# Input x handed over feature-major in column blocks; squares summed by products with ones, 1/rms multiplied in by VectorE and GpSimd; another order of the head

## The chip, the core and the metric

One Trainium2 chip, one of its cores. The metric is the device time of one execution in microseconds (us), the median of the runs shown. The engines are called as the profile calls them: PE (TensorE matmul), PEld (its weight load), DVE (VectorE), ACT (ScalarE), POOL (GpSimd), SP (SyncE, here only a queue of DMA issues). DVE, ACT and PE reach both on-chip memories, SBUF and PSUM; in this kernel POOL works on SBUF tiles only.

## The reference, cut to what matters

One decoder layer on 1024 prompt rows and 64 sample rows (8 sequences of 8), 1088 columns of work in all, 1024 features. What the change touches is the first line: the RMS norm of x, and the modulation by scale and shift, which come from a small product of the conditioning c with `w_ada`.

```python
shift, scale, gate = silu(c) @ w_ada + b_ada
h = x * rsqrt(mean(x * x, axis=-1) + 1e-6) * norm_g * (1 + scale) + shift
u_pool, z_pool, z_ssm, xBC, dt, g = split(h @ w_in)
P = (pool_mix(u_pool) * silu(z_pool)) @ w_pool_out
S = gated_rmsnorm(SSD(conv(xBC)) + D * xs, z_ssm) @ w_ssm_out
x = x + gate * ((sigmoid(g_pool) * P + sigmoid(g_ssm) * S) @ w_o)
y = rmsnorm(x, final_g)
```

All is float32. Large products are made of three products of halves: every operand is split into a rounded part ("hi") and the rest ("lo"), and hi*hi, hi*lo and lo*hi are summed in PSUM.

## The kernel before

h is wanted feature-major: 8 tiles k = 0..7 of 128 features (partitions) by 1088 columns, since the products with `w_in` sum over features. x arrives row-major. The 1088 columns are worked in three blocks, `BLK`: block 0 is 256 wide, block 1 384, block 2 448 (384 prompt columns and the 64 sample columns).

The head, `first()` (L837 and on), does the following. Nine loads bring x (L197, 128 rows each; the ninth is the 64 sample rows). `x_square` sums the squares of a row, on DVE (L204) or ACT (L206), into a column of `ss`; `x_root` (L210) and `x_unit` (L214) make 1/rms of 128 rows in one number per partition, and L219 puts these on the diagonal of a 128x128 matrix. `x_turn` (L231) multiplies a piece of x by that diagonal on PE: this turns the piece to feature-major and scales it at once. `x_copy` (L239 DVE, L241 ACT) brings it from PSUM into the tiles `tf[k]`. There are 64 pieces of 128x128 and 8 of 64 rows.

Beside this, `ada_load`, `ada_mm` (L277), `ada_out` (L284) and `ada_end` (L292 to L299) make shift and scale into the table `md`, in three parts: k 0 and 1, k 2 and 3, k 4 to 7. `h_make(block, ks)` makes h in place: for each k a rounded part on ACT (L323, for block 2 L332), the exact one on ACT for odd k (L325) or DVE for even k (L327), the rest `low` on DVE (L315). The sample columns have a scale and shift of their own for every sequence, two DVE operations of 64 columns per k (L330, L331). `products(block, ks)` (L866 to L868) are the first products with `w_in`: two column tiles of the gates g, whose weights `w_load` brings and `w_split` (L163 ACT, L166 DVE or POOL) splits. All of h and of these products done, `combine()` makes sums of h's quarters for the Strassen-like pairs that follow (L497 to L500 and others), `dt_block` (L727) makes dt, `gate_load` and `gate_mm` (L817, L823) make the gate of the residual. `gate_bias` (L827, L829) clears a tile `bg` on POOL and loads a bias into it; the gate loads stand behind these four loads on SP. Then the first pair starts (L595 to L597), and from there the same loop of pairs fills PE for the rest.

Order: `in_line` chains the instructions of `first()` on PE, ACT, DVE, POOL and SP in the order in which the code was written, so each of these queues runs the head exactly as written, one instruction behind the other, whatever is ready. Only the weights of the pairs (the L540 operations on DVE) are put between by the scheduler.

Of the kernel before, what the change touches and what calls it, by code (L numbers as in the profile page):

```python
# [8 lines left out]
F32 = mybir.dt.float32  # L9
# [11 lines left out]
P = 128  # L21
# [31 lines left out]
@with_exitstack  # L53
def tile_pool_ssd_step(
    ctx: ExitStack, tc: tile.TileContext,
    x_prompt, x_sample, state_pool, state_conv, state_ssm, state_turned, c_all,
    w_ada, b_ada, feat_vecs, w_in, w_first, w_dt, conv_vecs, dt_bias, a_log, skip_vecs,
    pool_w, w_pool_out, w_ssm_out, w_o, final_g,
    y_prompt, y_sample, new_pool_p, new_conv_p, new_ssm_p, new_pool_s, new_conv_s, new_ssm_s,
# [51 lines left out]
    def const(shape, name, dt=F32):  # L111
        return cp.tile(shape, dt, tag=name, name=name)
# [72 lines left out]
    xr = []
    xbig = [Y4(hs, F32), Y4(hs, F32)]
    ss = const([P, 9], "ss")
    nc.gpsimd.memset(ss, 1.0)
    rs = const([P, 9], "rs")
    dg = []  # L190
    hh_ = [None] * KT
    hl_ = [None] * KT

    def x_load(i):
        n = P if i < 8 else NS
        xt = R([P, D]) if i == 8 else xbig[i // 4][:, i % 4, :D]
        load(xt[:n], x_prompt[0, i * P:(i + 1) * P, :] if i < 8 else x_sample.rearrange("b t d -> (b t) d"))  # L197
        xr.append((xt, n))

    def x_square(i, eng):  # L200
        xt, n = xr[i]
        sqj = pa.tile([P, D], F32, tag="rawA", name=nm("sqj"), bufs=5)
        if eng is V:
            V.scalar_tensor_tensor(sqj[:n], xt[:n], 1.0, xt[:n], ALU.mult, ALU.mult, accum_out=ss[:n, i:i + 1])  # L204
        else:
            act(sqj[:n], xt[:n], AF.Square, accum_out=ss[:n, i:i + 1])  # L206

    def x_root(a, b):
        n = xr[a][1]
        act(rs[:n, a:b], ss[:n, a:b], AF.Sqrt, bias=eps[:n], scale=1.0 / D)  # L210

    def x_unit(a, b):
        n = xr[a][1]
        V.reciprocal(rs[:n, a:b], rs[:n, a:b])  # L214
        if not dg:
            dg.append(R())
        for i in range(a, b):
            n = xr[i][1]
            V.tensor_scalar(dg[0][:n, i * P:i * P + n], ident[:n, :n], rs[:n, i:i + 1], None, ALU.mult)  # L219

    tf = [None] * KT

    def x_turn(g3, k):

        if g3 == 0:
            tf[k] = tfp.tile([P, T], F32, tag="tf", name=nm("tf"), bufs=8)
        px = PB()
        c = 0
        for i in range((0, *XG)[g3], XG[g3]):
            xt, n = xr[i]  # L230
            mm(px[:, c:c + n], xt[:n, k * P:(k + 1) * P], dg[0][:n, i * P:i * P + n], start=True, stop=True)  # L231
            c += n
        return g3, k, px, c

    def x_copy(turned, eng):
        g3, k, px, c = turned
        o = BLK[g3][0]
        if eng is V:
            V.tensor_copy(tf[k][:, o:o + c], px[:, :c])  # L239
        else:  # L240
            act(tf[k][:, o:o + c], px[:, :c], AF.Copy)  # L241

    def x_turns(g3, ks):
        for k in ks:
            x_copy(x_turn(g3, k), nc.scalar if k % 2 else V)


    PARTS = ((0, 2), (2, 4), (4, 8))
# [3 lines left out]
    def ada_load(part, k):  # L252
        a, b = PARTS[part]
        w = (b - a) * P
        if part == 0:
            if k == 0:
                wtile[0] = Y4(hp, F32)
            t = wtile[0][:, k // 2, :D]
        else:
            if part == 2 or k % 2 == 0:  # L260
                wtile[part, k] = G((P, D))
            t = wtile[part, k if part == 2 else k - k % 2]
        if part == 2:
            load(t, w_ada[8 + k])
        else:
            if k % 2 == 0:
                load(t, w_ada[4 * part + k // 2])
            t = t[:, k % 2 * 512:k % 2 * 512 + 512]
        wraw[part, k] = t.rearrange("p (s c) -> p s c", s=2)
# [34 lines left out]
    def h_tile(k, j):  # L304
        if not hb:
            hb.extend(Y4(hp) for _ in range(2))
        return hb[j][:, k] if k < 4 else G((P, T), F32R)

    def h_make(g3, ks):

        o, w = BLK[g3]
        e = min(o + w, SEQ) - o

        def low(k):
            V.tensor_tensor(hl_[k][:, o:o + w], tf[k][:, o:o + w], hh_[k][:, o:o + w].bitcast(F32), ALU.subtract)  # L315
        for k in ks:
            if hh_[k] is None:
                hh_[k], hl_[k] = h_tile(k, 0), h_tile(k, 1)
            t = tf[k][:, o:o + w]
            hi = hh_[k][:, o:o + w]  # L320
            sc, sh = md[:, 8 + k], md[:, k]
            if e == w:
                act(hi, t, AF.Identity, scale=sc[:, 0:1], bias=sh[:, 0:1])  # L323
            if k % 2:
                act(t[:, :e], t[:, :e], AF.Identity, scale=sc[:, 0:1], bias=sh[:, 0:1])  # L325
            else:
                V.tensor_scalar(t[:, :e], t[:, :e], sc[:, 0:1], sh[:, 0:1], ALU.mult, ALU.add)  # L327
            if e < w:
                ts_ = t[:, e:w].rearrange("p (b i) -> p b i", i=8)
                V.tensor_tensor(ts_, ts_, sc[:, 1:9].unsqueeze(2).to_broadcast([P, NB, 8]), ALU.mult)  # L330
                V.tensor_tensor(ts_, ts_, sh[:, 1:9].unsqueeze(2).to_broadcast([P, NB, 8]), ALU.add)  # L331
                act(hi, t, AF.Copy)  # L332
            if k > ks[0]:
                low(k - 1)
        low(ks[-1])
# [502 lines left out]
    def first():  # L838
# [5 lines left out]
        def w_load(t, j):  # L844
            raws[t, j] = raw_()
            load(raws[t, j], w_first[t, j].rearrange("p (k c) -> p k c", c=P))
# [28 lines left out]
            act(buf[:, :n], banks[bi, t], AF.Sigmoid)  # L875
            store_(gs_d[t][:, o:o + n], buf[:, :n])

        for i in range(9):
            x_load(i)
        for k in range(KT):  # L880
            if k == KT - 2:
                w_load(0, 0)
                w_load(1, 0)
            ada_load(0, k)
        for k in range(KT):
            ada_load(1, k)
        for k in range(4):
            ada_load(2, k)
        late = late_loads()

        x_square(0, V)
        x_square(1, V)
        c_turn()
        x_root(0, 2)
        x_unit(0, 2)
        x_square(2, None)
        x_square(3, V)
        x_turns(0, range(2))
        x_square(4, None)
        x_turns(0, range(2, 4))  # L900
        x_root(2, 5)
        x_unit(2, 5)
        x_turns(0, range(4, 8))
        x_square(5, V)
        x_square(6, None)
        x_turns(1, range(4))
        x_square(7, V)
        x_square(8, None)
        x_turns(1, range(4, 6))
        x_root(5, 9)  # L910
        x_unit(5, 9)
        x_turns(1, range(6, 8))
        v_turn()
        x_turns(2, range(4))
        for k in range(6):
            ada_mm(0, k)
        x_turns(2, range(4, 5))
        w_split(0, 0)
        w_split(1, 0)
        ada_mm(0, 6)  # L920
        ada_mm(0, 7)
        mr = ada_out(0)
        x_turns(2, range(5, 6))
        ada_end(0, mr)
        turned = [x_turn(2, k) for k in (6, 7)]

        h_make(0, range(2))
        products(0, range(2))
        x_copy(turned[0], V)
        x_copy(turned[1], nc.scalar)  # L930
        h_make(1, range(2))
        for k in range(KT):
            ada_mm(1, k)
        products(1, range(2))
        h_make(2, range(2))
        w_load(0, 1)
        w_load(1, 1)
        for k in range(4, 8):
            ada_load(2, k)
# [1015 lines left out]
    for i in range(8):  # L1955
# [56 lines left out]
def _lay(name, i):  # L2012
# [69 lines left out]
```

## Time and profile before

| | us |
|---|---|
| three timed runs | 1239.1, 1239.18, 1239.2 (median 1239.18) |
| the profiled execution: its span, first to last instruction | 1238.8 (0.4 below the median of the runs; no other time of this execution is listed) |
| first product with `w_in` (L866) starts | 32.52 |
| first product of the first pair (L595) starts | 77.73 |
| mean granted TensorE clock over the span | 0.999 |

A row of the timeline gives the start, the time, the engine, the line, the operation, what it writes and reads, the shape and how many were merged; in brackets how long the engine had idled and who ended that. A row of the groups gives the engine, shape, count, then busy us and mean ns of one. A row of the windows gives a stretch, its length, and each engine's busy us and instructions in it.

### The profile page before, as it was taken

How to read it: one execution, taken by the hardware profiler on the slowest of the kernel's cores; microseconds unless marked ns; L12 is line 12 of the kernel's file. 1: busy time of each engine (PE TensorE's matmuls, PEld its weight loads, DVE VectorE, ACT ScalarE, POOL GpSimd, SP SyncE). 2: the span in 40 equal slices, each digit the busy share in tenths (PEclk: the TensorE clock that was granted, in tenths of full speed). 3: DMA queues.
4: the chain of work that ended last, by engine and by line, in shares of the span. 5: the costliest groups of instructions: out<-in, count | busy, mean ns of one | idle time of the engine just before them, and what ended most of it. 6: DMA issues, size and time to landing. Idle time of an engine off the chain costs nothing. (4 is left out here: it accounts for less than half of the span.)

```text
span 1238.8 us, 25381 instructions
## 1 busy us (share of the span) xinstructions
PE 1213.9 (98%) x9364; PEld 1145.0 (92%) x9364; DVE 909.2 (73%) x1579; ACT 692.8 (56%) x1611; POOL 678.0 (55%) x555
## 2 busy tenths in 40 slices
PE   6999999999999999999999999999999999999997
PEld 6779999999999999999898899999999999999786
DVE  4796688985989588975867775787767879666543
ACT  4665356565566556554554454877877768432111
POOL 1006669768898877774444465364565557456000
PEclk9999999999999999999999999999999999999999
DMA  9726445755556554453877775998665676485431
GB/s 363 290 99 226 145 161 148 188 190 170 164 173 208 158 168 146 169 179 114 251 248 211 231 223 183 329 306 298 192 203 176 195 228 198 143 296 167 153 111 51
DMA packets 183916, 243.25 MB, mean 196 GB/s; under 512 B 40808, under 2 KB 116912, under 8 KB 183792
## 3 DMA queue, kind: packets, MB, share of 16 engines
q1 hardware_dynamic: 132128, 167.90, 42.9%
q10 hardware_dynamic: 51664, 73.72, 17.6%
q8 instruction: 74, 1.21, 0.4%
q14 instruction: 50, 0.41, 0.1%
HBM read 166.96 MB, written 74.62 MB: 195 GB/s over the span
## 5 line engine op out<-in xcount | busy, mean ns | idle before, releaser
L166 POOL TENSOR_TENSOR wlo<-rawA,whi 128x512 fp32r<-128x512 f32 x120 | 187.5, 1569 | 143.1 <-DVE wlo L166 67.7
L166 POOL TENSOR_TENSOR wlo<-raw,whi 128x512 fp32r<-128x512 f32 x92 | 150.2, 1640 | 126.1 <-ACT whi L163 119.9
L360 PE MATMUL mm<-Y,whi 128*128 128x352 f32 (+1 forms) x480 | 160.1, 334 | 0.6
L361 PE MATMUL mm<-Y,whi 128*128 128x352 f32 (+1 forms) x480 | 157.1, 327 | 0.4 <-DVE Y L1485 0.4
L362 PE MATMUL mm<-Y,wlo 128*128 128x352 f32 (+1 forms) x480 | 157.1, 327 | 0.0
L595 PE MATMUL mm<-Y,whi 128*128 128x272 f32 x496 | 144.5, 292 | 1.0 <-ACT whi L163 0.8
L597 PE MATMUL mm<-Y,wlo 128*128 128x272 f32 x496 | 143.5, 290 | 1.3 <-DVE wlo L166 0.8
L596 PE MATMUL ps<-Y,whi 128*128 128x272 f32 x496 | 143.2, 289 | 0.0
L595 PE MATMUL ps<-Y,whi 128*128 128x272 f32 x496 | 142.8, 288 | 0.0
L597 PE MATMUL ps<-Y,wlo 128*128 128x272 f32 x496 | 142.8, 288 | 0.0
L596 PE MATMUL mm<-Y,whi 128*128 128x272 f32 x496 | 142.5, 287 | 0.0
L1031 DVE SCALAR_TENSOR_TENSOR GA<-GA,cvT,GA 128x1112 f32<-128x1112 f32 x72 | 128.4, 1786 | 0.7 <-ACT GA L1028 0.5
L163 ACT ACTIVATE whi<-rawA 128x512 fp32r<-128x512 f32 x125 | 77.8, 626 | 90.4 <-PE ps L596 51.1
L163 ACT ACTIVATE whi<-raw 128x512 fp32r<-128x512 f32 x96 | 58.7, 626 | 83.0 <-DVE raw L540 38.2
L595 PEld LDWEIGHTS mm<-Y,whi 128*128 128x128 f32 x496 | 93.6, 189 | 4.6 <-issue 2.4
L597 PEld LDWEIGHTS mm<-Y,wlo 128*128 128x128 f32 x496 | 93.1, 188 | 3.0 <-DVE wlo L166 1.2
L595 PEld LDWEIGHTS ps<-Y,whi 128*128 128x128 f32 x496 | 93.4, 188 | 1.7 <-issue 0.8
L596 PEld LDWEIGHTS mm<-Y,whi 128*128 128x128 f32 x496 | 93.5, 188 | 0.8 <-issue 0.6
L360 PEld LDWEIGHTS mm<-Y,whi 128*128 128x128 f32 x480 | 90.2, 188 | 4.1 <-DVE G L1861 2.3
L596 PEld LDWEIGHTS ps<-Y,whi 128*128 128x128 f32 x496 | 93.3, 188 | 0.2
L597 PEld LDWEIGHTS ps<-Y,wlo 128*128 128x128 f32 x496 | 93.2, 188 | 0.0
L361 PEld LDWEIGHTS mm<-Y,whi 128*128 128x128 f32 x480 | 90.2, 188 | 2.6 <-DVE Y L1485 0.9
(422 smaller groups left out, 3727.0 us busy)
## 6 DMA issues: line engine op xcount, KB each, us to landing
rawA<-in_w_in SPq DMA_DIRECT2D x62, 512.0 KB
dec<-acs_d SPq DMA_DIRECT2D x32, 512.0 KB
xbc<-GA ACTq DMA_DIRECT2D x24, 512.0 KB
xb<-xbc SPq DMA_DIRECT2D x32, 384.0 KB
pw<-in_w_ssm_out ACTq DMA_DIRECT2D x32, 256.0 KB
ws<-ph ACTq DMA_DIRECT2D x32, 256.0 KB
ws<-pw SPq DMA_DIRECT2D x32, 256.0 KB
hs<-in_state_turned SPq DMA_DIRECT2D x32, 256.0 KB
```

The costliest lines, as they stand in the source:

```text
L163: ins = act(hi[:, :, :ncols], raw[:, :, :ncols], AF.Copy)
L166: (eng or nc.gpsimd).tensor_tensor(lo[:, :, :ncols], raw[:, :, :ncols], hi[:, :, :ncols].bitcast(F32), ALU.subtract)
L360: mm(ps[:, :n], a, rh[k][:, o:o + n], start=(k == 0), stop=False)
L361: mm(ps[:, :n], a, rl[k][:, o:o + n], start=False, stop=False)
L362: mm(ps[:, :n], b, rh[k][:, o:o + n], start=False, stop=(k == nk - 1))
L595: mm(p, hi, ah, start=(k == 0), stop=False)
L596: mm(p, hi, al, start=False, stop=False)
L597: mm(p, lo, ah, start=False, stop=(k == 3))
L1031: V.scalar_tensor_tensor(d[:, :n], rp[:, k:k + n], cvT[:, 24 * k + mc:24 * k + mc + 1], d[:, :n], ALU.mult, ALU.add)
```

## The change

The host lays x out feature-major, in column blocks: for each partition first block 0 of the 8 feature tiles, then block 1, then block 2. `x_load` brings a block in two halves of four feature tiles. So nothing has to be turned; instead the sum of squares now runs over partitions. `x_square` squares half a block on ACT into the tile that later holds h. `x_fold` adds the two halves on DVE (blocks 1 and 2 only). `x_sum` multiplies the squares with a 128x128 matrix of ones on PE and adds up over k, which leaves the sum of every column in all 128 partitions: 8 products for block 0, 4 each for blocks 1 and 2. `x_root` takes the root on ACT and the reciprocal on DVE, now of 128 x 256, 384 and 448 numbers, and `x_unit` multiplies x by it: four of the eight feature tiles of a block on DVE, in two operations, four on POOL in one. The scale and shift of the sample columns go from DVE to POOL (`h_samples`), the second `w_split` too. `act(eps_root, ...)` loads the table of the root early.

```diff
+    tfb = tfp.tile([P, KT, T], F32, tag="tf", name="tf", bufs=1)
+    tf = [tfb[:, k] for k in range(KT)]
...
+            load(t, x_turned[:, c:c + 4 * n])
...
+    def x_square(bi, j):
+        o, n = BLK[bi]
+        act(tfb[:, 4 * j:4 * j + 4, o:o + n], xv[bi, j], AF.Square)
+
+    def x_fold(bi):
+        o, n = BLK[bi]
+        V.tensor_tensor(tfb[:, 0:4, o:o + n], tfb[:, 0:4, o:o + n], tfb[:, 4:8, o:o + n], ALU.add)
...
+    def x_sum(bi, ks):
...
         for k in ks:
-            x_copy(x_turn(g3, k), nc.scalar if k % 2 else V)
+            mm(sums_[bi][:, :n], ones, tf[k][:, o:o + n], start=(k == 0), stop=(k == (7 if bi == 0 else 3)))
+
+    def x_root(bi):
...
+        act(rsr[0][:, o:o + n], sums_[bi][:, :n], AF.Sqrt, bias=eps, scale=1.0 / D)
+        V.reciprocal(rsr[0][:, o:o + n], rsr[0][:, o:o + n])
+
+    def x_unit(bi, a, b, eng):
+        o, n = BLK[bi]
+        j = a // 4
+        eng.tensor_tensor(tfb[:, a:b, o:o + n], xv[bi, j][:, a - 4 * j:b - 4 * j],
+                          rsr[0][:, o:o + n].unsqueeze(1).to_broadcast([P, b - a, n]), ALU.mult)
...
+    def h_samples(a, b):
+        for m, op in ((8, ALU.mult), (0, ALU.add)):
+            for k in range(a, b):
+                tk = tf[k][:, SEQ:].rearrange("p (b i) -> p b i", i=8)
+                nc.gpsimd.tensor_tensor(tk, tk, md[:, m + k, 1:9].unsqueeze(2).to_broadcast([P, NB, 8]), op)
...
             if e < w:
-                ts_ = t[:, e:w].rearrange("p (b i) -> p b i", i=8)
-                V.tensor_tensor(ts_, ts_, sc[:, 1:9].unsqueeze(2).to_broadcast([P, NB, 8]), ALU.mult)
-                V.tensor_tensor(ts_, ts_, sh[:, 1:9].unsqueeze(2).to_broadcast([P, NB, 8]), ALU.add)
                 act(hi, t, AF.Copy)
```

The new order in `first()`, as written:

```python
        c_turn()
        act(eps_root, eps, AF.Sqrt)
        v_turn()
        x_square(0, 0)
        x_square(0, 1)
        x_sum(0, range(8))
        x_root(0)
        for k in range(KT):
            ada_mm(0, k)
        x_unit(0, 0, 2, V)
        mr = ada_out(0)
        ada_end(0, mr)
        x_square(1, 0)
        x_square(1, 1)
        h_make(0, range(2))
        x_fold(1)
        x_sum(1, range(4))
        w_split(0, 0)
        w_split(1, 0)
        x_unit(0, 4, 8, nc.gpsimd)
        x_root(1)
        x_unit(1, 0, 2, V)
        x_unit(0, 2, 4, V)
        products(0, range(2))
        x_square(2, 0)
        x_square(2, 1)
        h_make(1, range(2))
        x_fold(2)
        x_sum(2, range(4))
        x_root(2)
        x_unit(1, 4, 8, nc.gpsimd)
        x_unit(2, 0, 2, V)
        h_samples(0, 2)
        products(1, range(2))
        x_unit(1, 2, 4, V)
        x_unit(2, 2, 4, V)
        for k in range(KT):
            ada_mm(1, k)
        mr = ada_out(1)
        h_make(2, range(2))
...
        x_unit(2, 4, 8, nc.gpsimd)
        products(2, range(1))
...
        ada_end(1, mr)
        products(2, range(1, 2))
        h_samples(2, 4)
...
        products(2, range(2, 3))
        ada_end(2, mr)
        h_samples(4, 8)
```

What comes behind this stays as it was: on every engine the instructions after the head stand in the same order. The rows below are the programs' own order; line numbers of the changed kernel are some 8 to 11 lower than before (L228 is the new reciprocal, L212 `x_fold`, L233 `x_unit`, L302 `h_samples`, L310 and L322 are L315 and L327 before).

DVE before, from the scale and shift of k 0 and 1 to the end of `h_make(2)` for these: `tf` are the tiles of h, `Y` hi and lo, `md` scale and shift, `ps` PSUM.

```order
L296 TENSOR_TENSOR md<-ps_448,vT 128x18
L327 TENSOR_SCALAR tf_267<-tf_267,md 128x256
L315 TENSOR_TENSOR Y_464<-tf_267,Y_463 128x256
L315 TENSOR_TENSOR Y_464<-tf_272,Y_463 128x256
L239 COPY tf_304<-ps_453 128x448
L327 TENSOR_SCALAR tf_267<-tf_267,md 128x384
L315 TENSOR_TENSOR Y_464<-tf_267,Y_463 128x384
L315 TENSOR_TENSOR Y_464<-tf_272,Y_463 128x384
L327 TENSOR_SCALAR tf_267<-tf_267,md 128x384
L330 TENSOR_TENSOR tf_267<-tf_267,md 128x64
```

The same stretch of DVE in the changed kernel (`R_216` holds half of block 0 of x, `Y_225` block 1, `Y_232` block 2, `R_269` the reciprocal roots):

```order
L310 TENSOR_TENSOR Y_316<-tf,Y_315 128x256 x2
L212 TENSOR_TENSOR tf<-tf 128x4x384
L228 RECIPROCAL R_269<-R_269 128x384
L233 TENSOR_TENSOR tf<-Y_225,R_269 128x2x384
L233 TENSOR_TENSOR tf<-R_216,R_269 128x2x256
L322 TENSOR_SCALAR tf<-tf,md 128x384
L310 TENSOR_TENSOR Y_316<-tf,Y_315 128x384 x2
L212 TENSOR_TENSOR tf<-tf 128x4x448
L228 RECIPROCAL R_269<-R_269 128x448
L233 TENSOR_TENSOR tf<-Y_232,R_269 128x2x448
L233 TENSOR_TENSOR tf<-Y_225,R_269 128x2x384
L233 TENSOR_TENSOR tf<-Y_232,R_269 128x2x448
```

Fold, reciprocal and three multiplications of blocks 1 and 2 now stand between `low` of one block and `h_make` of the next, in one queue.

POOL before, between the split of the first weights and the first work for a later pair (`bg` is the tile of the gate's bias):

```order
L166 TENSOR_TENSOR wlo_425<-raw_232,whi_424 128x512
L166 TENSOR_TENSOR wlo_429<-raw_234,whi_428 128x512
L827 MEMSET bg 128x256
L166 TENSOR_TENSOR wlo_1279<-rawA_1274,whi_1278 128x512
L166 TENSOR_TENSOR wlo_1287<-rawA_1282,whi_1286 128x512
```

The same stretch of POOL in the changed kernel:

```order
L167 TENSOR_TENSOR wlo_334<-raw_230,whi_333 128x512
L233 TENSOR_TENSOR tf<-R_217,R_269 128x4x256
L233 TENSOR_TENSOR tf<-Y_225,R_269 128x4x384
L302 TENSOR_TENSOR tf<-tf,md 128x64 x4
L233 TENSOR_TENSOR tf<-Y_232,R_269 128x4x448
L302 TENSOR_TENSOR tf<-tf,md 128x64 x4
L167 TENSOR_TENSOR wlo_514<-raw_243,whi_513 128x512
L167 TENSOR_TENSOR wlo_518<-raw_245,whi_517 128x512
L302 TENSOR_TENSOR tf<-tf,md 128x64 x8
L819 MEMSET bg 128x256
```

The clearing of `bg` now stands behind all of POOL's work for h, the last part of which wants scale and shift of k 4 to 7. On SP, the loads of the gate's weights (`R` and `gk`, from `in_w_ada`) stand behind the loads into `bg`, before and now; in the changed kernel that queue reads:

```order
L521 DMA rawA_1156<-in_w_in 128x1024
L521 DMA rawA_1162<-in_w_in 128x1024
L821 DMA bg<-in_b_ada 9x256 x4
L809 DMA R_594<-in_w_ada 128x1024
L809 DMA R_596<-in_w_ada 128x1024
L809 DMA R_598<-in_w_ada 128x1024
L809 DMA gk_600<-in_w_ada 128x1024
```

Three more loads of a later pair's weights (the `rawA` rows) went ahead of the gate's loads; the order of the two kinds of rows behind them is as before.

More of the change, by code (lines that the diff above doesn't have):

```diff
@@ L55, in tile_pool_ssd_step @@
     ctx: ExitStack, tc: tile.TileContext,
-    x_prompt, x_sample, state_pool, state_conv, state_ssm, state_turned, c_all,
+    x_prompt, x_sample, x_turned, state_pool, state_conv, state_ssm, state_turned, c_all,
     w_ada, b_ada, feat_vecs, w_in, w_first, w_dt, conv_vecs, dt_bias, a_log, skip_vecs,
@@ L139, in tile_pool_ssd_step @@
         nc.gpsimd.memset(rc[:, t:t + 1], 1.0 / (t + 1))
+    eps_root = const([P, 1], "eps_root")
     c9 = const([P, KT, NB + 1], "c9")
@@ L182, in wcols @@
         return lambda: prep(w_in[0, :, c0:c0 + P], KT)
[L185 to L188, printed above, removed]
+    tfb = tfp.tile([P, KT, T], F32, tag="tf", name="tf", bufs=1)
+    tf = [tfb[:, k] for k in range(KT)]
     rs = const([P, 9], "rs")
-    dg = []
+    rsr = []
     hh_ = [None] * KT
     hl_ = [None] * KT
[L194 to L204, printed above, removed]
-        else:
[L206 to L241, printed above, removed]
@@ L243, in x_turns, with x_load @@
-    def x_turns(g3, ks):
-        for k in ks:
-            x_copy(x_turn(g3, k), nc.scalar if k % 2 else V)
+    xv = {}
+    def x_load(bi):
+        o, n = BLK[bi]
+        if bi == 0:
+            halves = [R((P, D)) for _ in range(2)]
+        else:
+            big = Y4(hs, F32).rearrange("p k t -> p (k t)")
+            halves = [big[:, j * 4 * n:(j + 1) * 4 * n] for j in range(2)]
+        for j, t in enumerate(halves):
+            c = KT * o + 4 * n * j
+            load(t, x_turned[:, c:c + 4 * n])
+            xv[bi, j] = t.rearrange("p (k t) -> p k t", t=n)
@@ new lines, in x_square @@
+    def x_square(bi, j):
[4 more added lines that the diff above has]
+        V.tensor_tensor(tfb[:, 0:4, o:o + n], tfb[:, 0:4, o:o + n], tfb[:, 4:8, o:o + n], ALU.add)
+    sums_ = {}
+    def x_sum(bi, ks):
+        o, n = BLK[bi]
+        if bi not in sums_:
+            sums_[bi] = PB()
+        for k in ks:
+            mm(sums_[bi][:, :n], ones, tf[k][:, o:o + n], start=(k == 0), stop=(k == (7 if bi == 0 else 3)))
@@ new lines, in x_root @@
+    def x_root(bi):
+        o, n = BLK[bi]
+        if not rsr:
+            rsr.append(R())
+        act(rsr[0][:, o:o + n], sums_[bi][:, :n], AF.Sqrt, bias=eps, scale=1.0 / D)
+        V.reciprocal(rsr[0][:, o:o + n], rsr[0][:, o:o + n])
+    def x_unit(bi, a, b, eng):
+        o, n = BLK[bi]
+        j = a // 4
+        eng.tensor_tensor(tfb[:, a:b, o:o + n], xv[bi, j][:, a - 4 * j:b - 4 * j],
+                          rsr[0][:, o:o + n].unsqueeze(1).to_broadcast([P, b - a, n]), ALU.mult)
@@ L876, in done @@
             store_(gs_d[t][:, o:o + n], buf[:, :n])
-        for i in range(9):
-            x_load(i)
+        x_load(0)
         for k in range(KT):
-            if k == KT - 2:
-                w_load(0, 0)
-                w_load(1, 0)
             ada_load(0, k)
+        x_load(1)
+        w_load(0, 0)
+        w_load(1, 0)
+        x_load(2)
         for k in range(KT):
             ada_load(1, k)
+        w_load(0, 1)
+        w_load(1, 1)
         for k in range(4):
@@ L889, in first @@
         late = late_loads()
-        x_square(0, V)
-        x_square(1, V)
         c_turn()
[L894 to L909, printed above, removed]
@@ L910, in first @@
-        x_root(5, 9)
-        x_unit(5, 9)
-        x_turns(1, range(6, 8))
-        v_turn()
-        x_turns(2, range(4))
-        for k in range(6):
-            ada_mm(0, k)
-        x_turns(2, range(4, 5))
+        act(eps_root, eps, AF.Sqrt)
+        v_turn()
+        x_square(0, 0)
+        x_square(0, 1)
+        x_sum(0, range(8))
+        x_root(0)
+        for k in range(KT):
+            ada_mm(0, k)
+        x_unit(0, 0, 2, V)
+        mr = ada_out(0)
+        ada_end(0, mr)
+        x_square(1, 0)
@@ L918, in first @@
+        x_square(1, 1)
+        h_make(0, range(2))
+        x_fold(1)
+        x_sum(1, range(4))
         w_split(0, 0)
         w_split(1, 0)
[L920 to L927, printed above, removed]
+        x_unit(0, 4, 8, nc.gpsimd)
+        x_root(1)
+        x_unit(1, 0, 2, V)
+        x_unit(0, 2, 4, V)
         products(0, range(2))
-        x_copy(turned[0], V)
@@ L930, in first @@
-        x_copy(turned[1], nc.scalar)
+        x_square(2, 0)
+        x_square(2, 1)
         h_make(1, range(2))
+        x_fold(2)
[4 more added lines that the diff above has]
+        h_samples(0, 2)
+        products(1, range(2))
+        x_unit(1, 2, 4, V)
+        x_unit(2, 2, 4, V)
         for k in range(KT):
             ada_mm(1, k)
-        products(1, range(2))
+        mr = ada_out(1)
         h_make(2, range(2))
-        w_load(0, 1)
@@ L937, in first @@
-        w_load(1, 1)
         for k in range(4, 8):
             ada_load(2, k)
+        x_unit(2, 4, 8, nc.gpsimd)
+        products(2, range(1))
         next(late)
-        mr = ada_out(1)
-        products(2, range(1))
         ada_end(1, mr)
         products(2, range(1, 2))
+        h_samples(2, 4)
         for bi in range(2):
@@ L949, in first @@
         h_make(2, range(2, 4))
-        w_split(0, 1, V)
-        w_split(1, 1, V)
+        w_split(0, 1)
+        w_split(1, 1)
         for k in range(KT):
@@ L1997, in tile_pool_ssd_step @@
     close(len(kept))
-_INS = ['x_prompt', 'x_sample', 'state_pool', 'state_conv', 'state_ssm', 'state_turned', 'c_all', 'w_ada', 'b_ada',
+_INS = ['x_prompt', 'x_sample', 'x_turned', 'state_pool', 'state_conv', 'state_ssm', 'state_turned', 'c_all', 'w_ada', 'b_ada',
         'feat_vecs', 'w_in', 'w_first', 'w_dt', 'conv_vecs', 'dt_bias', 'a_log', 'skip_vecs', 'pool_w',
@@ L2041, in _lay @@
     if name == "x_turned":
-        return _np.concatenate([i["x_prompt"][0], i["x_sample"].reshape(NS, D)]).T.reshape(KT, P, T)
+        x = _np.concatenate([i["x_prompt"][0], i["x_sample"].reshape(NS, D)]).T.reshape(KT, P, T).transpose(1, 0, 2)
+        return _np.concatenate([x[:, :, o:o + n].reshape(P, KT * n) for o, n in BLK], axis=1)
     a = i["state_ssm" if name == "state_turned" else name]
```

## The prediction

> **What bounds the kernel now.** First the page's busy shares, then the windows by stage, then TensorE's timeline through the head.
>
> ```profile
> PE 1213.9 (98%) x9364; PEld 1145.0 (92%) x9364; DVE 909.2 (73%) x1579; ACT 692.8 (56%) x1611; POOL 678.0 (55%) x555
> ```
>
> ```profile
> 32.52:77.73 45.21, 43.24 (x436) 31.66 (x435) 35.06 (x80) 29.99 (x54) 0.00 (x0) 1.00 0.67 242
> 130.00:1127.00 997.00, 991.51 (x7824) 954.20 (x7823) 773.54 (x1318) 594.13 (x1419) 635.65 (x498) 1.00 0.63 200
> ```
>
> From 130 us on PE is busy for 991.5 of 997 us, and there the instructions keep their order. So the rest takes its time wherever it starts, and the change is worth what it moves the start of the first pair, L595 at 77.73. In the head the places to compare are these:
>
> ```profile
> 9.29 12.27 PE L231 MATMUL ps<-R,Y 128*128 128x128 f32 x86 [9.29 <-DVE R L219]
> ...
> 32.52 0.39 PE L866 MATMUL mm<-Y,whi 128*128 128x256 f32 x1
> ...
> 40.51 0.36 PE L868 MATMUL ps<-Y,whi 128*128 128x448 f32 x1
> ...
> 56.63 1.07 PE L823 MATMUL ps<-R,scT 128*32 128x256 f32 x16
> ...
> 77.73 0.39 PE L595 MATMUL mm<-Y,whi 128*128 128x272 f32 x1 [0.41 <-ACT whi L163]
> ```
>
> ```profile
> 0.00:40.00 40.00, 21.25 (x144) 19.46 (x144) 1.00 0.90 336
> ```
>
> The last row is L231 alone: turning x holds PE for 21.25 us up to 32.52. When it is done, x lies scaled for all columns; from there PE waits little. The products of k 0 and 1 for all three blocks end at 40.7 (40.51 + 0.2), and 37.0 us later the pair starts.
>
> **Durations of what is added.** The squares are ACT passes, here for 1024 and 512 numbers:
>
> ```profile
> L206 ACT ACTIVATE sqj<-Y 128x1024 f32<-128x1024 f32 x3 | 3.1, 1046 | 0.0
> L163 ACT ACTIVATE whi<-raw 128x512 fp32r<-128x512 f32 x96 | 58.7, 626 | 83.0 <-DVE raw L540 38.2 <-PE ps L596 24.7 <-PE ps L597 10.9
> ```
>
> That is 0.82 ns a number: half a block costs 1.05, 1.47 and 1.68 us. On DVE and POOL:
>
> ```profile
> L1991 DVE TENSOR_TENSOR R<-R,m 128x1024 f32<-128x1024 f32 x7 | 8.6, 1225 | 0.2
> L1095 DVE RECIPROCAL h<-h 128x288 f32<-128x288 f32 x1 | 2.0, 1953 | 0.0
> L1994 DVE RECIPROCAL sso<-sso 128x1 f32<-128x1 f32 x7 | 1.2, 164 | 8.6 <-ACT sso L1993 8.6
> L1863 POOL TENSOR_TENSOR G<-G,m 128x1088 f32<-128x1088 f32 x6 | 15.2, 2539 | 3.6 <-DMA half<-gate_d 3.6
> L1467 POOL TENSOR_TENSOR sq_acc<-sq_acc,sz 128x64 f32<-128x64 f32 x3 | 1.0, 320 | 0.2
> ```
>
> ```profile
> 51.41 0.68 DVE L540 TENSOR_TENSOR raw<-rawA,rawA 128x512 f32<-128x512 f32 x1
> ```
>
> A DVE product of two tiles costs 0.68 for 512 and 1.06 ns for each further number: 0.95 for 768, 1.09 for 896, folds of 1.77 and 2.04. **The reciprocal costs (1953 - 164) / 287 = 6.2 ns a number**, six times that: 1.75, 2.55 and 2.95 us, 7.25 in all. Before, one number per row was enough; now every column's number is there 128 times over. POOL's multiplications, at 2.3 ns, take 2.4, 3.5 and 4.1 us, a sample operation 0.32. [...]
>
> The sums by ones are float32 products of two passes each. Of their kind, 16 passes of 384 columns, four side by side, start 1.29 us apart:
>
> ```profile
> 69.82 1.47 PE L727 MATMUL mm<-Y,dtw 128*32 128x384 f32 x16
> 71.11 1.47 PE L727 MATMUL mm<-G,dtw 128*32 128x384 f32 x16
> ```
>
> So a pass takes 1.29 / 4 = 0.32, 0.84 ns a column: 3.4 us for block 0, 2.6 and 3.0 for the others, 9.0 in place of 21.25.
>
> **Two things that decide.** POOL hardly worked in the head before. Later, DVE beside POOL reads so:
>
> ```profile
> 549.93 3.15 POOL L166 TENSOR_TENSOR wlo<-raw,whi 128x512 fp32r<-128x512 f32 x2 [4.98 <-ACT whi L163]
> ```
>
> ```profile
> 550.38 1.55 DVE L1096 TENSOR_TENSOR xw<-xw,h 128x288 f32<-128x288 f32 x1
> 551.85 0.42 DVE L613 TENSOR_TENSOR u<-u,mm 128x272 f32<-128x272 f32 x1
> 552.20 1.20 DVE L1097 TENSOR_TENSOR h<-xw 128x288 f32<-128x288 f32 x1
> ```
>
> 288 numbers should take 0.45; with two SBUF operands they take 1.55 and 1.20, which is one POOL operation waited out, then the work; the one with a PSUM operand (0.42) isn't held. I take it that a DVE operation on SBUF waits until POOL's running one ends, and the other way round. Here these are 3.5 and 4.1 us long.
>
> PE starts slowly. ACT's copies of turned tiles, which wait for PE:
>
> ```profile
> 11.40 0.38 ACT L241 ACTIVATE tf<-ps 128x256 f32<-128x256 f32 x1 [1.65 <-PE ps L231]
> 13.11 0.38 ACT L241 ACTIVATE tf<-ps 128x256 f32<-128x256 f32 x1 [0.29 <-PE ps L231]
> 14.36 0.39 ACT L241 ACTIVATE tf<-ps 128x256 f32<-128x256 f32 x1 [0.68 <-PE ps L231]
> 15.25 0.39 ACT L241 ACTIVATE tf<-ps 128x256 f32<-128x256 f32 x1 [0.51 <-PE ps L231]
> ```
>
> Eight passes lie between neighbours: 1.71 us at first, 0.89 later. After 9.29 idle us PE works at half rate for some 4.3 us (the granted clock reads 1.00 all the while), which loses 2.1.
>
> **The sum, first stage**, to the end of the products of k 0 and 1.
>
> ```profile
> 4.71 0.27 ACT L154 ACTIVATE scT<-c 128x72 f32<-128x72 f32 x1 [1.96 <-DMA c<-in_c_all]
> 7.12 1.28 ACT L210 ACT_TABLE_LOAD   x1 [2.14 <-DVE sqj L204]
> 8.42 0.30 ACT L210 ACTIVATE rs<-ss,eps 128x2 f32<-128x2 f32 x1
> ```
>
> ACT has its table and `eps_root` at 4.98 + 1.28 + 0.3 = 6.6. One square of block 0 is done at 7.6, PE adds 3.4 + 2.1 (the start) + 0.2 to drain: 13.3. Root 0.4, reciprocal 1.75: 15.5. Meanwhile PE makes shift and scale (1.9), ACT takes them out at 15.5 and squares block 1: 18.4. `h_make(0)` is three ACT passes, 1.6, and a last `low` of 0.45: 20.5. `x_fold(1)` 1.77: 22.2. Sum 2.8, root 0.5, reciprocal 2.55: 28.1. (The first product starts at 25, 7.5 before the old one.) Multiply k 0, 1: 29.0; now POOL takes its 3.5 for block 1, and DVE's next waits until 32.6. Another multiply 0.68, `h_make(1)` with 0.5, 0.55 and 0.55: 34.8. Fold 2.04, sum 3.2, root 0.55, reciprocal 2.95: 43.5. Multiply 1.09, then by turns with POOL 0.95, 0.32, 1.09, 0.32, 0.5 and 0.32: 48.1. ACT rounds (0.6), but POOL has begun its 4.1 us at 48.4, so both `low` of block 2 come at 53.7, and the last six products end at 55.2. Before: 40.7. **That is +14.5.** What hid the turning then, DVE and ACT idling for PE, hides nothing now: the chain runs fold, sum, root, reciprocal, block by block.
>
> **Second stage**, 37.0 us before. The gate's product waited for nothing:
>
> ```profile
> 29.21 0.31 POOL L827 MEMSET bg<- 128x256 f32 x1
> ```
>
> ```profile
> 0.81 4.64 SPq L197 DMA_DIRECT2D Y<-in_x_prompt  x8
> ...
> 41.94 2.31 SPq L829 DMA_DIRECT2D bg<-in_b_ada  x4
> ```
>
> ```profile
> 4.55 1.23 DVE L204 SCALAR_TENSOR_TENSOR sqj<-Y 128x1024 f32<-128x1024 f32 x1 [4.55 <-DMA Y<-in_x_prompt]
> 51.31 0.19 DVE L296 TENSOR_TENSOR md<-ps,vT 128x36 f32<-128x36 f32 x1
> ```
>
> Now `bg` is cleared behind eight sample operations that need the scale and shift of k 4 to 7. Those stood at 51.5, 10.8 behind the first stage's end. Eight turns of POOL (0.32) and DVE (some 0.3 of its own) make 4.9, the clearing 0.3, four issues on SP some 1.5 (2.31 with their waits), then a gate load, 3.7 from issue to use as the first load of x shows (0.81 to 4.55): 21.2. The gate's product stood 15.9 behind (56.63). PE waits 5.3 us, and the products queued behind it had no slack to give back. **+5.3.**
>
> **Restarts.** Between the sums PE has nothing for about 5 us before block 1's and 9 before block 2's. The nearest row is the start, after 9.29 idle: two more starts of 2.1, **+4.2**. [...]
>
> 14.5 + 5.3 + 4.2 = +24.0, counted in an execution with a span of 1238.8, 0.4 under the median of the runs. On that median, 1239.2: **1263 us**.
>
> **Rivals.** No restart after short gaps: 1259, chance 19%. For it: no gap inside the trace shows one; against it: the start does.
>
> Long POOL operations leave DVE alone: 3.5, 3.7, 1.0 and 2.3 us of waiting go, so +13.5 in all, 1253, chance 13%. For it: the held rows above stand beside POOL operations of 1.6 us only (3.15 for two), nothing longer is shown.
>
> More of the same: the reciprocal held by POOL too (1.4, where POOL multiplies block 0), and two restarts further on (4.2): 1269, chance 11%.
>
> The other side: PE bound the head, and the rest keeps pace. The first product is 7.5 earlier, block 2's sum takes 3.0 of it: 1234.7, chance 4%. It decides where block 2's h for k 0 and 1 is ready before PE has done block 1's products, about 33; the chain above says 48.
>
> No hold, no restart and the gate's loads in time together (about -10.5 - 4.2 - 5.3, with the reciprocal no dearer than a product) would leave it within 0.2%, what a measurement here can tell from no change: 3%. That the change does not do what it says has no chance: the order has no turning left.
>
> My own case has 50%. The range, 1248 to 1271, holds it and its three neighbours, the first two together too (1249); outside stay the other side, no change, and a little at each end. Slower 93%, same 3%, faster 4%.
>
> **What would show it.** Reciprocals of 1.7 to 3.0 us on DVE; DVE operations of 4 us beside POOL's; sums at half rate; first product near 25 to 27, the last of k 0 and 1 near 57 to 60; the clearing of `bg` after 70, and PE waiting for `R` from `in_w_ada` at its gate product. It is wrong if the first stage ends before 45 or the gate product waits for nothing.

## The result, and the profile after

| | us |
|---|---|
| changed kernel, four timed runs | 1265.91 to 1268.43, median 1267.1 |
| kernel before, four timed runs | 1239.1 to 1240.57, median 1239.19 |
| ratio | 1.0217, 95% interval 1.0203 to 1.0232 |
| profiled execution of the changed kernel | 1267.4, span 1265.7 |
| first product with `w_in` (L858 now) | 26.43 (before 32.52) |
| products of k 0 and 1 done, all blocks | 60.1 (before 40.7) |
| first product of the first pair (L587 now) | 103.85 (before 77.73) |

The change costs 27.9 us by the medians. Of all executions in this document one stands far out, 5822.85 us among the ten of e7 below; it is left out of e7's ratio, and e7's median, 1243.9, would be 1243.5 without it.

TensorE's timeline of the changed kernel, at the places that the prediction showed of before:

```profile
22.49 4.40 PE L221 MATMUL ps<-tf,ones 128*128 128x384 f32 x8 [6.15 <-DVE tf L212]
26.43 0.58 PE L858 MATMUL mm<-Y,whi 128*128 128x256 f32 x1
...
39.07 5.07 PE L221 MATMUL ps<-tf,ones 128*128 128x448 f32 x8 [10.80 <-DVE tf L212]
...
52.16 0.47 PE L858 MATMUL ps<-Y,whi 128*128 128x448 f32 x1 [4.05 <-ACT Y L324]
...
56.22 0.74 PE L860 MATMUL ps<-Y,whi 128*128 128x448 f32 x1 [3.39 <-DVE Y L310]
...
59.89 0.37 PE L860 MATMUL ps<-Y,whi 128*128 128x448 f32 x1
...
79.64 0.64 PE L815 MATMUL ps<-R,scT 128*32 128x256 f32 x8 [3.70 <-DMA R<-in_w_ada]
80.80 1.08 PE L815 MATMUL ps<-R,scT 128*32 128x256 f32 x8 [0.52 <-DMA R<-in_w_ada]
81.81 0.69 PE L858 MATMUL mm<-G,whi 128*128 128x384 f32 x1
...
103.85 0.39 PE L587 MATMUL mm<-Y,whi 128*128 128x272 f32 x1
```

The brackets tell the story: where PE turned x without a pause before, it now waits 6.15 and 10.80 us for DVE's folds, 4.05 and 3.39 for block 2's h, and at the gate 3.70 and 0.52 for weights. From the first pair on both traces need nearly the same, 1265.7 - 103.85 = 1161.9 and 1238.8 - 77.73 = 1161.1 us. So the loss is that of the pair's start, +26.1.

Who holds DVE is read from DVE's timeline and POOL's of the same kernel, side by side:

```profile
27.54 2.55 DVE L228 RECIPROCAL R<-R 128x384 f32<-128x384 f32 x1 [5.11 <-ACT R L227]
30.18 4.22 DVE L233 TENSOR_TENSOR tf<-Y,R 128x768 f32<-128x768 f32 x1
...
37.00 2.02 DVE L212 TENSOR_TENSOR tf<-tf 128x1792 f32<-128x1792 f32 x1
44.85 2.95 DVE L228 RECIPROCAL R<-R 128x448 f32<-128x448 f32 x1 [5.83 <-ACT R L227]
...
52.14 4.56 DVE L310 TENSOR_TENSOR Y<-tf,Y 128x448 fp32r<-128x448 f32 x2 [0.79 <-ACT Y L324]
```

```profile
30.17 3.42 POOL L233 TENSOR_TENSOR tf<-Y,R 128x1536 f32<-128x1536 f32 x1 [3.08 <-DVE R L228]
...
51.71 3.97 POOL L233 TENSOR_TENSOR tf<-Y,R 128x1792 f32<-128x1792 f32 x1
...
74.11 0.31 POOL L819 MEMSET bg<- 128x256 f32 x1
```

A multiply that should take 0.95 (0.96 in e4) shows 4.22, and ends 0.8 after POOL's operation of 3.42; two subtractions of 0.6 (0.63 each in e4) show 4.56 beside POOL's 3.97. The fold of block 2 (37.00) stands behind the held multiply and `h_make(1)` in DVE's queue, though its squares were done at 30.7. And `bg` is cleared at 74.11 only. SP issues the loads into `bg` right behind that, then the gate's weights, which PE has at 79.64:

```profile
74.44 1.40 SPq L821 DMA_DIRECT2D bg<-in_b_ada  x4
75.89 1.30 SPq L809 DMA_DIRECT2D R<-in_w_ada  x3
```

The windows of the changed kernel (after the stretch and its length come busy us of PE, PEld, DVE, ACT, POOL; the third number from the end is the granted clock) show what the groups don't:

```profile
22.00:27.00 5.00, 4.51 (x11) 2.69 (x12) 0.44 (x1) 0.07 (x1) 5.00 (x3) 0.63 1.05 406
39.00:44.00 5.00, 4.93 (x9) 2.44 (x10) 0.02 (x1) 0.00 (x0) 0.00 (x0) 0.63 0.00 0
52.00:60.00 8.00, 4.45 (x13) 3.61 (x14) 5.50 (x8) 2.41 (x6) 4.82 (x5) 0.57 0.50 164
80.00:87.00 7.00, 6.48 (x32) 5.39 (x25) 6.04 (x11) 5.09 (x9) 0.00 (x0) 0.52 0.90 342
```

Before, the clock was 1.00 in every microsecond from 8 to 110. Now it is 0.5 in most of each of these stretches, which lie behind PE's gaps of 6.15, 10.80, 4.05 and 3.39, and 3.70 and 0.52 us.

### The profile page after: what moved, and what is told of

It reads as the page before. It is cut to its first block, busy times and chain, and to the rows that moved or that the text cites. A ratio compares the mean times of both kernels' runs of the same rounds, so it can differ in the third digit from the quotient of the medians.

```text
span 1265.7 us, 25122 instructions
## 1 busy us (share of the span) xinstructions
PE 1213.3 (96%) x9252; PEld 1138.6 (90%) x9252; DVE 913.5 (72%) x1538; ACT 692.6 (55%) x1598; POOL 698.0 (55%) x575
## 5 line engine op out<-in xcount | busy, mean ns | idle before, releaser
L167 POOL TENSOR_TENSOR wlo<-raw,whi 128x512 fp32r<-128x512 f32 x94 | 154.0, 1647 | 128.5 <-ACT whi L164 120.9
L587 PE MATMUL mm<-Y,whi 128*128 128x272 f32 x496 | 144.6, 292 | 1.0 <-DVE GA L605 0.7
L587 PE MATMUL ps<-Y,whi 128*128 128x272 f32 x496 | 142.9, 288 | 0.0
L587 PEld LDWEIGHTS mm<-Y,whi 128*128 128x128 f32 x496 | 93.6, 189 | 4.6 <-issue 3.3
L587 PEld LDWEIGHTS ps<-Y,whi 128*128 128x128 f32 x496 | 93.4, 188 | 1.7 <-DVE xw L1240 0.8
```

Source lines behind the costliest of these rows:

```text
L167: (eng or nc.gpsimd).tensor_tensor(lo[:, :, :ncols], raw[:, :, :ncols], hi[:, :, :ncols].bitcast(F32), ALU.subtract)
L587: mm(p, hi, ah, start=(k == 0), stop=False)
```

## The experiments

The first five take one suspected cost away from the changed kernel, each alone; the others put these edits together. The kernel before ran beside each on the same chip, with medians from 1239.5 to 1240.9.

| run | pair starts | profiled span | median | ratio to before, interval |
|---|---|---|---|---|
| the change | 103.85 | 1265.7 | 1267.1 | 1.0217 (1.0203 to 1.0232) |
| e1, `bg` cleared early | 96.31 | 1258.6 | 1260.6 | 1.0170 (1.0155 to 1.0186) |
| e2, PE filled | 97.66 | 1259.1 | 1260.8 | 1.0168 (1.0152 to 1.0183) |
| e3, no reciprocal | 98.86 | 1263.3 | 1260.8 | 1.0176 (1.0154 to 1.0198) |
| e4, no multiplications on POOL | 95.49 | 1261.2 | 1262.2 | 1.0169 (1.0136 to 1.0202) |
| e5, no folds | 91.93 | 1252.3 | 1253.8 | 1.0102 (1.0086 to 1.0117) |
| e6, e1 + e2 + e4 | 85.71 | 1249.4 | 1251.0 | 1.0094 (1.0059 to 1.0128) |
| e7, e6 and no folds | 81.58 | 1242.7 | 1243.9 | 1.0025 (1.0015 to 1.0035) |
| e8, head reordered | 82.00 | 1242.6 | 1243.2 | 1.0032 (1.0022 to 1.0042) |
| e9, POOL beside the reciprocal | 78.89 | 1238.9 | 1242.5 | 1.0015 (1.0006 to 1.0024) |

The start of the pair is the sharper measure: the stretch behind it is the same work in each, and took from 1160.0 (e9) to 1165.7 us (e4) in the profiled executions (e4's four runs lie from 1256.2 to 1264.2). It is itself good to about 1 us only: the first sum by ones, the same work in all of these kernels, ended between 13.1 (e9) and 14.7 (e2).

**e1.** The clearing of `bg` and its loads stand ahead of the second `w_split`.

```diff
+        bg = gate_bias()
         w_split(0, 1)
...
-        bg = gate_bias()
         for k in range(4):
             gate_load(k)
```

> The clearing of bg and its four loads are written ahead of the second w_split, so that POOL clears bg before the sample operations of k 4 to 7 and SP issues the gate's loads before three loads of a later pair; nothing else is changed. Gate theory: the changed kernel's PE idles 3.7 and 0.5 us before the gate's products (75.8 to 80.8) and then works at half clock until 87.1; all of that goes, 5 to 7 us, to about 1261. Rival: the gate's loads would be late without the clearing too (their buffers, the queue on SP), and the time stays at 1267.

The pair starts 7.5 us earlier. TensorE's timeline of e1 has no wait at the gate, and the clock stays at 1.00 from 61 us on:

```profile
75.70 1.07 PE L815 MATMUL ps<-R,scT 128*32 128x256 f32 x16
```

The waits were 4.2, so 3.3 of the 7.5 lay in the slow clock behind them, which went with them. A POOL operation of 0.31 us, queued behind the wrong work, cost more, by the pair's start, than the three reciprocals together (5.0, below).

**e2.** Idle products in PE's gaps, as in

```diff
+    def idle_mm(bank, n):
+        for _ in range(n):
+            mm(bank[:, :P], ones, ident, start=True, stop=True)
...
             sums_[bi] = PB()
+            idle_mm(sums_[bi], IDLE.get(bi, 0))
```

> The changed kernel, with idle products of 128 columns (ones times the identity, into a bank that the next real product clears) in PE's gaps: 24 before the sum of block 1, 44 before that of block 2, 15 and 13 before and between the first products of block 2, 15 before the gate's first product. No wait is removed. Clock theory: the two sums, the products of block 2 and those behind the gate's run at full clock, 1.4 + 1.6 + 1.6 + 2.6 = 7 us less, about 1260, with a granted clock of 1.00 throughout. Rival: the products are slow for another reason, or the waits behind them take up what they gain: 1267 with the clock at 1.00.

6.2 us by the pair, 6.3 by the medians, a little under the 7 expected; e2's first sum ended 0.9 later than the change's. The granted clock is 1.00 in every microsecond from 8 to 110. PE's timeline of e2 shows the sums at 2.85 and 3.27 us, which took 4.40 and 5.07:

```profile
23.41 2.85 PE L228 MATMUL ps<-tf,ones 128*128 128x384 f32 x8 [0.80 <-DVE tf L212]
...
38.47 3.27 PE L228 MATMUL ps<-tf,ones 128*128 128x448 f32 x8 [0.99 <-DVE tf L212]
```

Nothing was taken away; PE only did more. So the slow products of the changed kernel came from PE's own idling, 6.15 and 10.80 us ahead of the two sums where e2 has 0.80 and 0.99, not from x arriving or from the kind of product.

**e3.** Leaves the reciprocals out, as its expectation says: the line `V.reciprocal(...)` in `x_root` goes.

> Leaves out the three reciprocals: x is multiplied by the root itself. Chain theory (fold, sum, root, reciprocal in series set the first stage): 1.75 + 2.55 + 2.95 = 7.25 us less, about 1260. Rival: DVE had the time, since the stage waits for x, ACT or POOL: within 1.5 us of 1267.

5.0 by the pair, 6.3 by the medians: on the path, but not with their whole 7.25. The first of the three, 1.75, was hidden behind ACT's squares of block 1, for which `h_make(0)` waits in both kernels. So the fold of block 1 comes no earlier without it. DVE's row of the changed kernel, then that of e3:

```profile
20.69 1.75 DVE L212 TENSOR_TENSOR tf<-tf 128x1536 f32<-128x1536 f32 x1
```

```profile
21.53 1.75 DVE L212 TENSOR_TENSOR tf<-tf 128x1536 f32<-128x1536 f32 x1
```

It comes 0.8 later, about as much as e3's first sum, the same work in both, took longer (6.53 for 5.61). 7.25 less these two is 4.7. POOL's hold cost as much as before, but fell on another operation. With the reciprocal gone, POOL's multiplication of block 1 still begins beside DVE's work, and holds the next multiply in place of the first (3.93 for one of 0.68):

```profile
28.85 0.96 DVE L232 TENSOR_TENSOR tf<-Y,R 128x768 f32<-128x768 f32 x1 [5.57 <-ACT R L227]
29.73 3.93 DVE L232 TENSOR_TENSOR tf<-R,R 128x512 f32<-128x512 f32 x1
```

**e4.** POOL's three multiplications go to DVE, into stretches where it idled.

```diff
-        x_unit(0, 4, 8, nc.gpsimd)
...
         x_fold(1)
+        x_unit(0, 4, 8, V)
...
-        x_unit(1, 4, 8, nc.gpsimd)
...
         x_fold(2)
+        x_unit(1, 4, 8, V)
...
-        x_unit(2, 4, 8, nc.gpsimd)
...
         h_make(2, range(2, 4))
+        x_unit(2, 4, 8, V)
```

> The three multiplications of four feature tiles go from POOL to DVE, behind the fold of the next block (blocks 0 and 1) and behind h_make(2, 2..4) (block 2), where DVE idles 5.1, 5.8 and 3.5 us in the changed kernel. Hold theory: DVE's multiply of block 1 (4.22 us in the trace) and the low of block 2 (4.56 for two) lose their waits for POOL, 3.3 and 3.4 us; both lie on the path: about 6.5 less, 1260.5. Rival (a long POOL operation doesn't hold DVE; these are waits for something else): DVE has 5 us more to do and nothing is won, 1267 to 1270.

The pair starts 8.4 earlier, though DVE has 5 us more to do; the medians differ by 4.9, with runs far apart. DVE's timeline of e4 has the same instructions at their own length:

```profile
29.76 0.96 DVE L233 TENSOR_TENSOR tf<-Y,R 128x768 f32<-128x768 f32 x1
...
48.35 0.63 DVE L310 TENSOR_TENSOR Y<-tf,Y 128x448 fp32r<-128x448 f32 x1 [0.80 <-ACT Y L324]
49.62 0.63 DVE L310 TENSOR_TENSOR Y<-tf,Y 128x448 fp32r<-128x448 f32 x1 [0.65 <-ACT Y L324]
```

4.22 became 0.96 and 4.56 became 1.26 of work. POOL's operations of 3.42 and 3.97 us did hold DVE, by 3.3 us each, and moving half of the multiplications to POOL made the head longer.

**e5.** `x_fold` goes, and `x_sum` takes all eight tiles of blocks 1 and 2.

```diff
-        x_fold(1)
-        x_sum(1, range(4))
+        x_sum(1, range(8))
...
-        x_fold(2)
-        x_sum(2, range(4))
+        x_sum(2, range(8))
```

> The folds of blocks 1 and 2 go from DVE; PE sums all eight feature tiles of squares instead of four (4 x 2 passes of 0.32 and 0.375 more). Chain theory: a sum then waits for ACT's squares alone, which are done at 18.7 and 30.7, and not for DVE's queue (fold of block 1 at 20.7, of block 2 behind h_make(1) at 37.0); the reciprocal of block 2 moves from 44.9 to about 37.5, the time falls by about 7.5 to 1259.5. Rival (only the folds' own time counts): 1.75 + 2.02 less on DVE, 2.8 more on PE, 1266.

13.3 by the medians, 11.9 by the pair: more than either theory gave. DVE's timeline of e5 has block 2's reciprocal at 32.99, which was 44.85:

```profile
24.16 2.56 DVE L228 RECIPROCAL R<-R 128x384 f32<-128x384 f32 x1 [2.69 <-ACT R L227]
...
32.99 2.95 DVE L228 RECIPROCAL R<-R 128x448 f32<-128x448 f32 x1
```

The folds' 3.8 us of DVE are the smaller part. A sum no longer waits for DVE's turn but for ACT's squares, so the sum of block 1 starts at 18.09 (22.49), and since PE idles for 1.04 and 0.40 us ahead of them in place of 6.15 and 10.80, both sums run with the granted clock at 1.00, which the expectation had left out. Two slow stretches are left, at the products of block 2 (the clock at 0.50 from 41.0 to 47.8) and behind the gate (from 68.3 to 75.1).

**e6 and e7.** The parts together; no new lines, but with 24, 28 and 15 idle products in e6 and 10, 8 and 6 in e7.

> Early clearing of bg, no multiplications on POOL, and PE filled (24 idle products before the sum of block 1, 28 before that of block 2, 15 before the products of block 2) together. If the three losses are separate: from the run without POOL's multiplications, whose pair starts at 95.5, about 5 go for the gate's wait and the slow clock behind it, 4.6 for the other slow stretches: pair near 86, 1248 to 1250. If they cover the same wait, no more than the best of them: 1260.

> As e6, and the folds left out (sums over eight tiles); 10, 8 and 6 idle products. Chain theory: block 2's reciprocal no later than 36, the products of k 0 and 1 done near 45, the pair at 80 to 82: 1241 to 1245, still behind the kernel before, whose turning left the same products done at 40.7. Rival (with the chain cut, the head is bound by PE and the early start of the first product shows): under 1238.

Pair at 85.71 and at 81.58, both where they were expected; e6's median, 1251.0, is 1 above its range. The parts don't add up in full. Alone, those of e6 gave 7.5 + 6.2 + 8.4 = 22.1, together they give 18.1; the folds gave 11.9 alone and 4.1 on top of e6. So they share some of the loss: the slow clock behind the gate goes with e1's edit and with e2's, and the slow sums go with e2's and with e5's. In e7 the products of k 0 and 1 end near 45; before, at 40.7.

**e8.** The order of the head rewritten, here its core; the edits of e1, e4 and e5 are in it too:

```diff
+        x_square(1, 0)
+        x_square(1, 1)
         mr = ada_out(0)
         ada_end(0, mr)
...
+        x_square(2, 0)
+        x_square(2, 1)
...
         x_root(1)
         x_unit(1, 0, 2, V)
+        x_sum(2, range(8))
         products(0, range(2))
...
         h_make(2, range(2, 4))
+        x_unit(1, 4, 8, V)
+        x_unit(2, 4, 8, V)
```

> No folds, no multiplications on POOL, bg cleared early, no idle products; and the head's order is changed: squares of block 1 ahead of ada_out(0), squares and sum of block 2 ahead of the root of block 1 and of the products of block 0, and DVE's multiplications for k 2 to 7 behind h_make(2) of k 0 and 1. Chain theory: the sum of block 2 starts near 25.4 instead of 27.4 and PE has no gap over 3 us, so the clock stays at 1.00; block 2's reciprocal starts near 32.5, its products for k 0 and 1 end near 41, as in the kernel before, and the pair starts at 77 to 79: 1238 to 1241, within 0.2% of the kernel before. Rival (x of block 2 lands too late for squares at 22, or DVE's queue takes up what is won): pair at 81, 1243 to 1245, like e7.

The rival came true. The products of k 0 and 1 do end at 41.4, but the two multiplications put behind `h_make(2)` of k 2 and 3 now meet POOL's second `w_split`. DVE's rows of e8, then POOL's:

```profile
48.56 4.78 DVE L233 TENSOR_TENSOR tf<-Y,R 128x1536 f32<-128x1536 f32 x2
53.27 0.18 DVE L285 TENSOR_TENSOR md<-ps,vT 128x36 f32<-128x36 f32 x1
53.48 1.03 DVE L288 TENSOR_TENSOR md<-md,vT 128x36 f32<-128x36 f32 x1
```

```profile
48.58 5.88 POOL L167 TENSOR_TENSOR wlo<-raw,whi 128x512 fp32r<-128x512 f32 x2 [5.75 <-ACT whi L164]
```

3.8 us of work on DVE and 2.5 on POOL (its length where nothing is beside it, in the changed kernel at 66.05) take each other's turns. The last scale and shift come later for it, PE waits 1.97 at 55.3, and works at half clock from 57.8 to 61.2, as it did from 37.3 to 40.7 behind a wait of 2.46. The expectation had it at 1.00 with no gap over 3 us; the gaps behind the start were 2.46 at most, and the clock fell all the same. In e7, with one of 2.50, it had not.

**e9.** On top of e8, POOL takes one multiplication back, at a place of its own, and 8 idle products stand ahead of block 2's products:

```diff
         act(rsr[0][:, o:o + n], sums_[bi][:, :n], AF.Sqrt, bias=eps, scale=1.0 / D)
+        if bi == 2:
+            nc.gpsimd.tensor_copy(junk, rsr[0][:, o:o + 1])
+            x_unit(1, 4, 8, nc.gpsimd)
         V.reciprocal(rsr[0][:, o:o + n], rsr[0][:, o:o + n])
```

> As e8, but POOL multiplies k 4 to 7 of block 1 again, held back by a copy of one number per row from block 2's root, so that it runs beside the reciprocal of block 2 (31.4 to 34.4); and 8 idle products ahead of block 2's products. In the trace of e5 a POOL multiplication of 2.39 us and a reciprocal of 2.56 us ran beside each other at their own lengths (24.08 to 26.72). If the reciprocal, with one SBUF operand, isn't held: it takes 2.95, DVE's next multiply waits under 1 us, e8's collision of DVE with the second w_split (4.78 us for 3.8) shrinks, the products of k 0 and 1 end near 41, the pair starts at 77 to 79, 1238 to 1241. Rival (it is held, either side waiting the other out): reciprocal or POOL operation of 6 us, products 3 later, 1243 or more.

DVE's timeline of e9, then POOL's:

```profile
30.47 2.95 DVE L239 RECIPROCAL R<-R 128x448 f32<-128x448 f32 x1 [0.21 <-POOL junk L237]
33.51 1.40 DVE L244 TENSOR_TENSOR tf<-Y,R 128x896 f32<-128x896 f32 x1
```

```profile
30.39 3.58 POOL L244 TENSOR_TENSOR tf<-Y,R 128x1536 f32<-128x1536 f32 x1
```

The reciprocal takes its 2.95 and POOL runs through it; only the multiply behind it waits 0.3 (1.40 for 1.09 in e8). The pair starts at 78.89, 1.2 after the kernel before and 3.1 ahead of e8. Part of this is luck: the profiled execution was the fastest of e9's eleven (1240.61), and its first sum, which no edit touched, ended 1.2 sooner than e8's. By the medians e9 gains 0.6 on e8. Its median, 1242.5, is above the 1241 that was expected, beside 1240.7 of the kernel before in the same rounds, and the ratio's interval just leaves 1.0. One spell at half clock is left in it (42.0 to 45.4). With the other losses found here mended, host-turned x comes to about 0.15% behind turning x on PE, and doesn't beat it.

## Why the prediction was right, and where it was off

The forecast was 1263 (1248 to 1271, 93% slower); 1267.1 was measured. Profile against profile it was +24.0 for the pair's start, and +26.1 came.

**First stage, +14.5 with +4.2 for restarts: right, with some luck in the restarts.** 55.2 + 4.2 = 59.4 was forecast for the end of the products of k 0 and 1, 60.1 came. The two sums lost less to the slow clock than the 4.2, but block 2's products lost something to it that the sum didn't have (below). Reciprocals of 1.75, 2.55 and 2.95 and folds of 1.75 and 2.02 stand as worked out, the first product falls in the forecast's 25 to 27. In one detail it went the other way round: POOL, not DVE, had the first turn at 30.17, so the held operation was the multiply of block 1 rather than the next. e3, e4 and e5 show the three parts of the chain (reciprocal, hold, queue behind the fold) each on the path, the reciprocal of block 0 apart.

**POOL holds DVE: right**, and the rival without it (1253) falls with e4's rows. The rows tell more closely which operations were held: those with two operands in SBUF (4.22 for 0.96, two of 0.63 in 4.56). A reciprocal, with one, took its 2.95 beside POOL's 3.58 in e9. In e8, with POOL at work until 54.46, the addition at 53.27 of one operand in PSUM and one in SBUF took its 0.18, and the next, with both in SBUF, 1.03 (0.20 in the changed kernel, at 69.84).

**Second stage, +5.3: right in kind, its parts sized otherwise.** The stage took 103.85 - 60.1 = 43.8 in place of 37.0. The wait itself was 4.2 (forecast 5.3), from the clearing of `bg` as forecast, behind sample operations that took 4.05 in place of 4.9; e1 shows it.

**Restarts, +4.2: too small.** This is the term that was mis-sized. The sum had two slow starts of 2.1; the runs showed four. Against the same passes at full clock: 3.94 - 2.57 = 1.4 in the sum of block 1 (8 passes of 0.32), 4.56 - 3.0 = 1.6 in block 2's, some 1.6 in its products at 56, and some 2.5 behind the gate (16 products mostly 0.32 apart for 0.175), about 7 in all. Those of the two sums were smaller than the start's 2.1, which stood behind 9.29 idle us: that gaps of 5 and 9 us would cost as much each was not shown, and behind 6.15 and 10.80 us it was the 1.4 and 1.6. The two behind further gaps stood only in the rival "more of the same". 1267.1 lies nearer to that rival's 1269 than to 1263; the other half of it, a reciprocal held by POOL, didn't come (1.75 for block 0). e2 gives 6.2 for the same thing, with a first sum that ended 0.9 later. The rival without restarts (1259) falls. The prediction's remark that the granted clock reads 1.00 all the while holds for the start alone; behind later gaps the profile shows the 0.5.

**The rest moves along: right**, to 0.8 us. **The other side** (PE bound the head, so less PE work is a gain) was not met: PE's first product came 6.1 earlier, and won nothing, because block 2's h for k 0 and 1 was ready at 56 and not at 33.

Together: +0.7 in the first stage, -1.1 in the gate's wait, +2.5 in the clock behind it and +0.8 in the rest are the 2.9 by which the spans' difference (26.9) exceeds the forecast. The last 1.0 up to the medians' 27.9 is a matter of which execution was profiled: in every execution shown with both, the time is 1.7 above the span, so the profiled one of before, span 1238.8, took about 1240.5, which fits the highest of its four runs, 1240.57.

## What to carry to other kernels

Work taken off the bounding engine is a gain only if what replaces it can be ready earlier; here it was a chain through four in-order queues, and a link could wait longer for its queue's turn than its own work takes (the fold of block 2 waited from 30.7 to 37.0 for 2.02 of work). Before giving POOL a long operation, look at what stands behind it in POOL's queue, and at which operations of DVE have two SBUF operands beside it: one of 3.42 us made a multiply of 0.96 last 4.22 here, while beside a reciprocal, in e9, one of 3.58 cost DVE 0.3. And a gap on PE cost twice in the changed kernel: the wait, and some 1.4 to 2.5 us at half clock behind it. So in the sum each new gap may need a restart of its own: half clock also came behind gaps of 2.46 and 1.97 us in e8 and of 1.77 in e9, though not behind one of 2.50 in e7.

## What the runs showed of the hardware

In the profiled execution of the changed kernel the granted clock changed at 18.84, 25.66, 32.48, 42.72, 52.96, 59.80, 80.28 and 87.10 (from the granted clock microsecond by microsecond). These are 6.82, 6.82, 10.24, 10.24, 6.84, 20.48 and 6.82 us apart, which is 2, 2, 3, 3, 2, 6 and 2 times 3.41. Windows of the changed kernel laid on that grid, PE's busy time first:

```profile
46.10:49.55 3.45, 2.01 (x65) 1.69 (x64) 3.36 (x3) 0.28 (x1) 0.49 (x1) 1.00 0.48 135
49.55:52.96 3.41, 0.68 (x2) 0.30 (x2) 2.62 (x4) 1.34 (x3) 3.41 (x5) 1.00 0.95 370
...
80.28:83.69 3.41, 2.89 (x15) 2.08 (x15) 2.58 (x5) 3.30 (x5) 0.00 (x0) 0.50 0.96 371
83.69:87.10 3.41, 3.41 (x12) 3.41 (x11) 3.27 (x6) 1.60 (x4) 0.00 (x0) 0.50 0.82 306
```

and two of e9:

```profile
38.56:41.97 3.41, 1.57 (x8) 0.96 (x6) 2.67 (x8) 1.19 (x3) 1.20 (x5) 1.00 0.29 97
41.97:45.38 3.41, 3.07 (x13) 3.07 (x14) 2.68 (x6) 2.41 (x4) 0.23 (x1) 0.50 0.31 65
```

After the window with PE busy for 2.01 us the clock stayed at 1.00; after those with 0.68 and, in e9, even 1.57 us it fell. It rose again after 3.41 and, in e9, 3.07 us, and not after 2.89. The gap in e9's first window was of 1.77 us. Whether the busy time of such a window is what decides, no run shows.
